# A two-layer encoder on eight cores: sine table in small steps, weights in smaller pieces, a new store layout, and fewer waits at the end

## The chip, the cores and the metric

One Trainium2 chip, eight cores, one sequence of the batch on each; no core waits for another. The time is device time of the slowest core in microseconds (us). A program on all eight cores has a slower state, whatever the kernel: in some executions the cores of one die, or of both, show a lower granted TensorE clock and take several per cent longer. The engines are called PE (TensorE), ACT (ScalarE), DVE (VectorE), POOL (GpSimd) and SP (SyncE); POOL and SP also issue the transfers, each on a ring of its own.

## The reference, cut to what matters

```python
# x: [8, 2048, 2048]; layer 0 gated linear attention, layer 1 latent attention
for i in range(2):
    y = gla_mixer(x, ...) if i == 0 else mla_mixer(x, positions, ...)
    x = layer_norm(alpha * x + y, ln_g[i], ln_b[i])

def gla_mixer(x, ...):      # 4 heads, chunks of 64 frames
    q, k, v, z, a_lr = split(x @ w_in)
    log_a = log_sigmoid(a_lr @ w_a2 + b_a) / 16
    state = decay * state + k^T v;  o = q state            # chunk by chunk
    return (rms_norm(o) * silu(z)) @ w_out

def mla_mixer(x, positions, ...):   # 16 heads; rotary part of 64, by sin/cos of position * inv_freq
    ...                             # chunk-causal softmax attention
    return (o * silu(z)) @ w_out
```

The sine and cosine of the positions are needed only in layer 1, which begins when the row tiles of layer 0 are done (after some 1050 us).

## The kernel before

The kernel is written as a list of operations; a scheduler in Python, with a cost model of engines and transfers, puts them in order on the five engines. An engine's queue is run in that order.

The sine table of 2048 positions is made in four blocks at the very start of the list, with a bonus in priority of 600, from one buffer for the positions (`trg`) and two for the result (`tra`):

```python
tra = [P.sbuf("tra", ..., [2, 512], F32) for j in range(2)]

def trig(tb, after=()):
    posi, ang, tk, ti = trg
    full = tra[tb % 2]
    P.dma(SP, posi, pos_d[:, tb * 512:(tb + 1) * 512], after=after)
    P.copy(ang, posi)
    P.ts(ang, ang, ropec[:, 0:1], None, ALU.mult)
    for f, shift in enumerate((0.0, PI / 2)):
        ...                              # nine DVE steps of 128x512: range reduction
    P.act(full, full, AF.Sin)            # ACT
    for f in range(2):
        P.dma(SP, cs_s[tb][f], full[:, f, :], ...)   # to HBM, for layer 1
```

At the end of layer 0 the output projection reads one row tile (`ogt`, 128 of the 2048 positions) per 64 matmuls, while the weights of the next stage (`wckv`) are loaded in two pieces of 1 MB. In layer 1 each head's output is transposed on PE, copied by DVE to a staging buffer (`ogS`, four of them) and stored by SP; beside that, in one of four head groups, POOL loads the output weights:

```python
P.copy(ogS[nh % 4], t)                                                   # DVE
P.dma(SP, ogT_s[1][4 * qb:4 * qb + 4, :, head, :].rearrange("i p t -> p i t"), ogS[nh % 4], ...)
...
if g == 1:
    load_slab(wout2[qb], m_wout[qb], after=[lastexp[0]])                 # four slabs
```

At the end SP waits for the last transfer on every semaphore, one after another:

```python
for o in last.values():                 # 120 of them
    h.wait_ge(nd[o.sem], o.cnt)
```

The softmax here doesn't subtract the row's maximum and nothing guards it: scores larger than these inputs give would overflow.

## Time and profile before

| | before |
|---|---|
| time, median of the first 4 runs | 2347.21 us (2277.78 to 2676.58) |
| profiled run (fast) | 2277.78 us |
| cores 0, 3, 4, 6 | 2275.0, 2276.2, 2275.5, 2273.0 us |
| cores 1, 2, 5, 7 | 2255.3, 2255.2, 2255.1, 2253.5 us |
| PE busy, slowest core | 96% |
| last matmul to the end, core 3 | 2259.9 to 2276.2 us |

The first four runs held slow ones, so their median says little; in all 18 runs taken beside the changed kernel the median is 2278.07 us. Read the profile as a stream of 12880 matmuls with a few holes in it: PE is the bound, so the question is only where it stands still and what it stands for. The prediction shows those lines. One line that it did not look at belongs here, the DRAIN at the end of POOL's queue on core 3, an instruction that every engine's queue ends with (name, count, duration in ns three times, first and last start):

```profile
L400 POOLq DRAIN  x1: 8664/8664/8664, 2265.3 to 2265.3; - x1
```

It is over at 2273.98, 2.3 us before the end: it costs nothing here.

### The profile page before, as it was taken

Reading aid. Unit: us, or ns where it says so; the run is one execution under the profiler, and the core shown is the slowest. Engines: PE = TensorE matmul, PEld = TensorE weight load, DVE = VectorE, ACT = ScalarE, POOL = GpSimd, SP = SyncE. Lnnn points to the kernel's source line nnn. Section 1 sums busy time; section 2 is a strip of 40 time slices with the busy share of each in tenths; the row PEclk is TensorE's granted clock in tenths of the full one; section 3 lists DMA queues with packets and bytes.
Section 4 is the critical chain, followed back from the end, with each engine's and each line's share of the span. In section 5 each row is a group of like instructions: output and inputs, shape, how many; then the busy total and the mean of one; then the engine's idle time right before and its main releaser. Section 6 shows DMA issues by size and latency. Waiting matters only on the chain.

```text
span 2276.2 us, 32728 instructions; the slowest of 8 cores (2253.5 to 2276.2 us)
## 1 busy us (share of the span) xinstructions
PE 2184.6 (96%) x12880; PEld 1100.2 (48%) x12880; DVE 978.0 (43%) x1819; ACT 836.0 (37%) x1539; POOL 344.4 (15%) x275
## 2 busy tenths in 40 slices
PE   6399999999999999999999999999989999999997
PEld 2144444444444444444444444446656666545553
DVE  1553444444344445666433222215343443565556
ACT  0354445444444442332432111114635555312220
POOL 2010111110111102333201111110000000032223
PEclk9799999999999999999999999999999999999998
DMA  9820600420152255545924344342266322434333
GB/s 162 153 65 10 128 12 10 82 58 10 28 107 49 49 142 150 183 156 182 185 58 113 101 124 129 100 138 75 61 146 141 91 65 77 165 141 147 134 126 121
DMA packets 132246, 237.59 MB, mean 104 GB/s; under 512 B 42368, under 2 KB 100096, under 8 KB 120832
## 3 DMA queue, kind: packets, MB, share of 16 engines
q1 hardware_dynamic: 119712, 164.20, 22.5%
q0 software_dynamic: 12384, 71.29, 18.4%
q8 instruction: 106, 1.74, 0.3%
q14 instruction: 44, 0.36, 0.1%
HBM read 229.15 MB, written 77.59 MB: 135 GB/s over the span
## 4 chain that ended last, share of the span: by engine, by line
PE 92%; DMA 5%; DVE 1%; ACT 1%; issue 0%; POOL 0%; DVEq 0%; SPq 0%; POOLq 0%
PE psum_all L153 89%; PE psum_all L159 2%; DMA trg<-pos_bc 2%; DMA ogT_s<-ogS 1%; DMA cs_s<-tra 1%; DMA xT<-xT 1%; DMA ogt<-ogT_s 1%; DVE slot_ap L188 0%; DVE xrE L188 0%; ACT L179 0%; ACT sig L179 0%; ACT tra L179 0%; DVE tra L188 0%; DVE trg L212 0%; ACT glp L179 0%
## 5 line engine op out<-in xcount | busy, mean ns | idle before, releaser
L153 PE MATMUL psum_all<-wsl,xT 128*128 128x512 bf16 x2048 | 471.6, 382 | 21.5 <-DMA wsl<-g_slab 19.9
L179 ACT ACTIVATE pT<-psum_all 128x1024 bf16<-128x1024 f32 (+1 forms) x320 | 284.6, 895 | 361.8 <-PE psum_all L153 361.2
L153 PEld LDWEIGHTS psum_all<-wsl,xT 128*128 128x128 bf16 x2048 | 195.8, 99 | 243.7 <-issue 36.4
L153 PE MATMUL psum_all<-wout,ogt 128*128 128x512 bf16 x1024 | 235.4, 382 | 5.3 <-DMA ogt<-ogT_s 5.3
L153 PE MATMUL psum_all<-xT,wsl 128*128 128x512 bf16 x1024 | 231.9, 379 | 0.0
L153 PE MATMUL psum_all<-wz,x1T 128*128 128x512 bf16 x1024 | 230.3, 379 | 0.0
L153 PE MATMUL psum_all<-wout,ogtE 128*128 128x512 bf16 x1024 | 226.3, 379 | 0.0
L153 PE MATMUL psum_all<-qnD,kC 128*128 128x512 bf16 (+3 forms) x640 | 221.5, 348 | 0.0
L153 PE MATMUL psum_all<-qrD,kr 128*128 128x512 bf16 (+3 forms) x640 | 218.6, 348 | 0.0
L153 PEld LDWEIGHTS psum_all<-vC,pT 128*128 128x128 bf16 x2176 | 148.6, 98 | 69.6 <-issue 0.7
L153 PE MATMUL psum_all<-vC,pT 128*128 128x129 bf16 x2176 | 179.8, 220 | 0.0
L153 PEld LDWEIGHTS psum_all<-wz,x1T 128*128 128x128 bf16 x1024 | 100.2, 98 | 120.8
L153 PEld LDWEIGHTS psum_all<-wout,ogtE 128*128 128x128 bf16 x1024 | 99.3, 98 | 117.5 <-issue 0.8
L153 PEld LDWEIGHTS psum_all<-wout,ogt 128*128 128x128 bf16 x1024 | 98.1, 98 | 113.5 <-issue 9.6
L188 POOL TENSOR_TENSOR slot_ap<-zs,gout 128x512 bf16<-128x512 bf16 x64 | 74.9, 1171 | 512.7 <-DVE zs L188 512.6
L153 PEld LDWEIGHTS psum_all<-xT,wsl 128*128 128x128 bf16 x1024 | 98.2, 98 | 110.3
L188 POOL TENSOR_TENSOR xrE<-xrE,lnbE 128x1024 f32<-128x1024 f32 (+1 forms) x31 | 84.2, 2737 | 421.3 <-DVE xrE L188 421.1
L179 ACT ACTIVATE zst<-psum_all 128x512 bf16<-128x512 f32 x64 | 38.2, 597 | 251.5 <-PE psum_all L153 251.5
L188 POOL TENSOR_TENSOR xr<-xr,lnb 128x1024 f32<-128x1024 f32 x32 | 88.3, 2777 | 145.5 <-DVE xr L188 145.5
L195 DVE SCALAR_TENSOR_TENSOR state<-state,cc,psum_all 128x512 f32<-128x512 f32 x112 | 78.7, 743 | 62.8 <-PE psum_all L153 59.3
L212 DVE CAST vC<-psum_all 128x512 bf16<-128x512 f32 x64 | 44.3, 692 | 118.2 <-PE psum_all L153 118.2
L175 ACT CAST slot_ap<-psum_all 128x512 bf16<-128x512 f32 x64 | 36.8, 586 | 133.1 <-PE psum_all L153 132.7
(142 smaller groups left out, 2590.8 us busy)
## 6 DMA issues: line engine op xcount, KB each, us to landing
wsl<-g_slab POOLq DMA_DIRECT2D x18, 1024.0 KB, 11.0
xr<-x SPq DMA_DIRECT2D x16, 1024.0 KB, 6.6
x_s<-xr SPq DMA_DIRECT2D x32, 512.0 KB, 3.5
xrE<-x_s SPq DMA_DIRECT2D x16, 1024.0 KB, 7.6
out<-xrE SPq DMA_DIRECT2D x30, 512.0 KB, 2.6
ogT_s<-ogst SPq DMA_DIRECT2D x64, 128.0 KB, 1.8
wout<-g_wout POOLq DMA_DIRECT2D x8, 1024.0 KB, 13.0
ogt<-ogT_s SPq DMA_DIRECT2D x16, 512.0 KB, 3.9
```

The source lines that it names most:

```text
L153: return self.add(PE, lambda: t.matmul(out, lhsT, rhs, start=start, stop=stop, skip_group_check=skip), [lhsT, rhs], [out], n / 2.4 + 3, af ...
L159: return self.add(PE, lambda: t.transpose(out, in_, idn), [in_, idn], [out], 56)
L175: f = lambda: a.copy(out, in_)
L179: f = lambda: a.activation(out, in_, func, bias=bias, scale=scale)
L188: return self.add(e, lambda: h.tensor_tensor(out, a, b, op), [a, b], [out], self.dcost(n) if e == DVE else 110 + 2.05 * n, after=after)
L195: return self.add(DVE, lambda: v.scalar_tensor_tensor(out, in0, s, in1, op0, op1), reads, [out], self.dcost(n))
L212: return self.add(e, lambda: h.tensor_copy(out, in_), [in_], [out], 130 + n * (0.65 if e == DVE else 1.2))
```

## The change

Its intent: take the sine work out of the way of the stream's start, take the pressure off the transfers at two places where PE waits, and shorten the end. Cut to its core:

```diff
 # scheduler's model of a transfer issued by SP
-    spfree = max(free[e] + 1200, spfree) + o.nbytes / 170.0
-    bwfree = max(bwfree, spfree) if bwfree < free[e] else bwfree + o.nbytes / self.BW
+    busy = bwfree > free[e] + 500
+    spfree = max(free[e] + 1200, spfree) + o.nbytes / (110.0 if busy else 300.0)
+    if busy:
+        bwfree += o.nbytes / self.BW
 # end: four waits after the last store, the others before it
-    for o in last.values():
+    for o in final[-4:]:
         h.wait_ge(nd[o.sem], o.cnt)
 # sine table: one operation at a time
-def trig(tb, after=()):
+def trig_steps():
+    ...                                   # the same operations, a yield after each
-P.bias = 600
-for t4 in range(4):
-    trig(t4, [ld])
-P.bias = 0
+trig = trig_steps()
 ...                                       # in head 0, per half-tile step from token block 1 on
+                if h == 0 and tb > 0:
+                    anchor = next(q.i for q in reversed(P.ops) if q.e == PE)
+                    n0 = len(P.ops)
+                    for _ in range(4):
+                        next(trig, None)
+                    for q in P.ops[n0:]:
+                        q.deps.add(anchor)
 # layer 0's row tiles: the loads of x split from those of ogt and issued earlier (cut)
 # next stage's weights in eight pieces
-            load_slab(wckv, m_slab[1])
+        if 3 <= i < 11:
+            q = 2 * (i - 3)
+            P.dma(POOL, wckv[:, q:q + 2, :], m_slab[1][:, q:q + 2, :], after=[P.ops[-1]])
 # layer 1's outputs: six staging buffers, one 1 KB row per partition
-    ogS = [... [4, 128] ... for j in range(4)]
+    ogS = [... [512] ... for j in range(6)]
-        P.dma(SP, ogT_s[1][4 * qb:4 * qb + 4, :, head, :].rearrange("i p t -> p i t"), ogS[nh % 4],
+        P.dma(SP, ogT_s[1][qb, :, head, :], st,
 # layer 1's output weights: 16 pieces over two head groups
-            if g == 1:
-                load_slab(wout2[qb], m_wout[qb], after=[lastexp[0]])
+        if g in (1, 2) and pr[0][0] == 0 and hh % 2 == 0:
+            n = 8 * (g - 1) + 2 * qb + hh // 2
+            P.dma(POOL, wout2[n // 4][:, 4 * (n % 4):4 * (n % 4) + 4, :], ..., after=[lastexp[0]])
```

With the sine part the load of the fourth weight slab (a block of 2 MB), whose place in memory the sine buffers use until then, moves from head 0's first token block to its last (cut here).

More of the change, by code (lines that the diff above doesn't have):

```diff
@@ L368, in ref @@
                 return (nd[d.sem] if d.dma else esem[d.e]), d.cnt
+            final = [o for o in self.order if o.dma and not o.succ]
             def body(e):
@@ L373, in run @@
                         w = {}
+                        if final and o is final[-4]:
+                            for f in final[:-4]:
+                                h.wait_ge(nd[f.sem], f.cnt)
                         for d in o.waits:
@@ L391, in run @@
                     if e == SP:
-                        last = {}
-                        for o in self.order:
-                            if o.dma:
-                                last[o.sem] = o
-                        for o in last.values():
+                        for o in final[-4:]:
                             h.wait_ge(nd[o.sem], o.cnt)
@@ L442, in build_program @@
     out_d = nc.dram_tensor("out", [NT, 128, D], F32, kind="ExternalOutput").ap()
-    ogT_s = [dscr(f"ogT{l}_s", [NT, 128, KC, 128], BF16) for l in range(2)]
+    ogT_s = [dscr("ogT0_s", [NT, 128, KC, 128], BF16), dscr("ogT1_s", [4, 128, KC, 512], BF16)]
     x1_s = dscr("x1_s", [NT, 128, D], F32)
@@ L682, in build_program @@
     tra = [P.sbuf("tra", W[2] + 8192 + 4096 * j, [2, 512], F32) for j in range(2)]
-    def trig(tb, after=()):
+    def trig_steps():
         posi, ang, tk, ti = trg
-        full = tra[tb % 2]
-        P.dma(SP, posi, pos_d[:, tb * 512:(tb + 1) * 512], after=after)
-        P.copy(ang, posi)
-        P.ts(ang, ang, ropec[:, 0:1], None, ALU.mult)
-        for f, shift in enumerate((0.0, PI / 2)):
-            a2 = full[:, f, :]
-            P.ts(a2, ang, shift, None, ALU.add)
-            P.ts(tk, a2, 1.0 / TWO_PI, None, ALU.mult)
-            P.copy(ti, tk)
-            P.copy(tk, ti)
-            P.stt(a2, tk, -TWO_PI, a2, ALU.mult, ALU.add)
-            P.ts(tk, a2, PI, -TWO_PI, ALU.is_gt, ALU.mult)
-            P.tt(DVE, a2, a2, tk, ALU.add)
-            P.ts(tk, a2, -PI, TWO_PI, ALU.is_lt, ALU.mult)
-            P.tt(DVE, a2, a2, tk, ALU.add)
-        P.act(full, full, AF.Sin)
-        for f in range(2):
-            P.dma(SP, cs_s[tb][f], full[:, f, :], dw=[("cs", tb)])
+        P.dma(SP, posi, pos_d[:, 0:512])
+        for _ in range(12):
+            yield
+        for tb in range(4):
+            full = tra[tb % 2]
+            P.copy(ang, posi)
+            yield
+            P.ts(ang, ang, ropec[:, 0:1], None, ALU.mult)
+            if tb < 3:
+                P.dma(SP, posi, pos_d[:, (tb + 1) * 512:(tb + 2) * 512])
+            yield
+            for f, shift in enumerate((0.0, PI / 2)):
+                a2 = full[:, f, :]
+                P.ts(a2, ang, shift, None, ALU.add)
+                yield
+                P.ts(tk, a2, 1.0 / TWO_PI, None, ALU.mult)
+                yield
+                P.copy(ti, tk)
+                yield
+                P.copy(tk, ti)
+                yield
+                P.stt(a2, tk, -TWO_PI, a2, ALU.mult, ALU.add)
+                yield
+                P.ts(tk, a2, PI, -TWO_PI, ALU.is_gt, ALU.mult)
+                yield
+                P.tt(DVE, a2, a2, tk, ALU.add)
+                yield
+                P.ts(tk, a2, -PI, TWO_PI, ALU.is_lt, ALU.mult)
+                yield
+                P.tt(DVE, a2, a2, tk, ALU.add)
+                yield
+            P.act(full, full, AF.Sin)
+            for f in range(2):
+                P.dma(SP, cs_s[tb][f], full[:, f, :], dw=[("cs", tb)])
+            yield
@@ L750, in build_program @@
             prev = (h, tb)
-            if h == 0 and tb == 0:
+            if h == 0 and tb == 3:
+                for _ in trig:
+                    pass
                 load_slab(sl_w(3), g_slab[3])
@@ L767, in __init__, with load @@
             self.nb = 0
-        def load(self, i):
+        def load(self, i, what="ox"):
             l = self.layer
-            P.dma(SP, self.ogt[i % len(self.ogt)], ogT_s[l][i], dr=[(f"ogT{l}", i, h) for h in range(4 if l == 0 else 16)])
-            P.dma(SP, self.xr[i % len(self.xr)], self.src[i], dr=[("x1", i)] if l else [])
+            src = ogT_s[1][i // 4][:, :, (i % 4) * 128:(i % 4) * 128 + 128] if l else ogT_s[0][i]
+            if "o" in what:
+                P.dma(SP, self.ogt[i % len(self.ogt)], src, dr=[(f"ogT{l}", i, h) for h in range(4 if l == 0 else 16)])
+            if "x" in what:
+                P.dma(SP, self.xr[i % len(self.xr)], self.src[i], dr=[("x1", i)] if l else [])
         def proj(self, i, n):
@@ L822, in build_program @@
     xr = [P.sbuf("xr", S + 8192 * j, [D], F32) for j in range(3)]
-    P.dma(SP, lng, lng_d[0])
-    P.dma(SP, lnb, lnb_d[0])
     ln0 = LN(0, x_d, x1_s, wout, lng, lnb, xr, ogt, stats, [0, 1])
@@ L845, in build_program @@
     ln0.load(0)
+    P.dma(SP, lng, lng_d[0])
+    P.dma(SP, lnb, lnb_d[0])
+    ln0.load(1, "x")
     for i in range(NT):
         if i + 1 < NT:
-            ln0.load(i + 1)
+            ln0.load(i + 1, "o")
         for n in range(4):
@@ L856, in build_program @@
                 x1_transposes(i - 1)
+            if n == (1 if i else 3) and i + 2 < NT:
+                ln0.load(i + 2, "x")
         ln0.norm(i)
@@ L1035, in build_program @@
     ogD = [P.sbuf("ogD", S + 16384 + 1024 * j, [4, 128], BF16) for j in range(4)]
-    ogS = [P.sbuf("ogS", S + 20480 + 1024 * j, [4, 128], BF16) for j in range(4)]
-    rsD = [P.sbuf("rsD", S + 24576 + 64 * j, [2], F32) for j in range(4)]
+    ogS = [P.sbuf("ogS", S + 20480 + 1024 * j, [512], BF16) for j in range(6)]
+    rsD = [P.sbuf("rsD", S + 27648 + 64 * j, [2], F32) for j in range(4)]
     o[0] = M
@@ L1160, in og_out @@
             P.tr(t[:, s, :], ogD[nh % 4][:, s, :])
-        P.copy(ogS[nh % 4], t)
+        st = ogS[nh % 6]
+        P.copy(st, bankb(b)[:, 0:512])
         head = 4 * g + hh
-        P.dma(SP, ogT_s[1][4 * qb:4 * qb + 4, :, head, :].rearrange("i p t -> p i t"), ogS[nh % 4],
+        P.dma(SP, ogT_s[1][qb, :, head, :], st,
               dw=[("ogT1", 4 * qb + s, head) for s in range(4)])
@@ L1242, in build_program @@
         p = scores(g, qb, hh, pr)
+        if g in (1, 2) and pr[0][0] == 0 and hh % 2 == 0:
+            n = 8 * (g - 1) + 2 * qb + hh // 2
+            P.dma(POOL, wout2[n // 4][:, 4 * (n % 4):4 * (n % 4) + 4, :], m_wout[n // 4][:, 4 * (n % 4):4 * (n % 4) + 4, :],
+                  after=[lastexp[0]])
         inflight.append((w, p))
```

## The prediction

> **What bounds the kernel now.** I read the page first, then the cores, then what TensorE (PE) waited for, and only then the stretches in which those waits lie.
>
> ```profile
> PE 2184.6 (96%) x12880; PEld 1100.2 (48%) x12880; DVE 978.0 (43%) x1819; ACT 836.0 (37%) x1539; POOL 344.4 (15%) x275
> PE   6399999999999999999999999999989999999997
> PEclk9799999999999999999999999999999999999998
> ```
>
> PE is busy 96% of the 2276.2 us, at full clock but for one slice near the start and the last one. The change removes no matmul, so all it can win is the other 92 us and what the clock loses after a gap. The waits of PE on this core (core 3, the slowest) say where those are:
>
> ```profile
> PE psum_all L153 <- ACT slot_ap L175: 34.5, 1, 34.5
> PE psum_all L153 <- DMA wsl<-g_slab: 19.9, 5, 12.8
> PE psum_all L153 <- DVE ogS L212: 9.6, 1, 9.6
> PE psum_all L153 <- DMA ogt<-ogT_s: 5.3, 1, 5.3
> ```
>
> Four entries are 69 us; the tail after the last matmul (2260 to 2276) is 16 more. The first 12.8 us of the weight wait is the start itself, which stays. The timeline around 100 us tells what the 34.5 us are:
>
> ```profile
> 97.97 0.43 DVE L202 TENSOR_SCALAR tra<-trg 128x512 f32<-128x512 f32 x1 [8.38 <-DMA cs_s<-tra]
> 100.69 1.06 ACT L179 ACTIVATE tra<-tra 128x1024 f32<-128x1024 f32 x1 [19.14 <-DVE tra L188]
> 101.66 2.03 ACT L175 CAST slot_ap<-psum_all 128x512 bf16<-128x512 f32 x4
> 102.85 5.72 PE L153 MATMUL psum_all<-xT,walr 128*16 128x512 bf16 x16 [34.49 <-ACT slot_ap L175]
> ```
>
> The rotary sine table stands in ScalarE's (ACT) queue ahead of the copies that empty PE's banks. ACT waited 19.14 us for VectorE (DVE), which waited for the store of the table before last, because there are two table buffers. PE had ended its third block at 68.4 us and got its bank only at 102.85.
>
> Cores 0, 3, 4 and 6 take 2273 to 2276 us, the other four 2253 to 2255. Core 1's waits start with
>
> ```profile
> PE psum_all L153 <- ACT slot_ap L175: 27.4, 1, 27.4
> ```
>
> and have 2.6 us for ogt and none for ogS. So the slow four carry two waits that the fast four hardly have, and the change must help the slow ones.
>
> **What the Trainium skill says.** (1) "TensorE: Matmul & The Clock Gate", Part 1: after an idle window of about 3.4 us PE falls to half clock and needs about as long to come back. The trace agrees: the windows after the ogt and ogS waits have granted clocks of 0.52 and 0.50:
>
> ```profile
> 875.00:880.00 5.00, 3.82 (x10) 1.34 (x11) 0.00 (x0) 0.00 (x0) 0.22 (x1) 0.52 0.85 320
> 1695.00:1700.00 5.00, 4.25 (x20) 2.28 (x21) 3.09 (x9) 0.42 (x1) 0.00 (x0) 0.50 1.01 293
> ```
>
> So each wait of over 3.4 us costs some 2 to 3 us on top of itself. (2) The same page, "Engine queue depths": ACT's and DVE's queues are strict FIFO; the 34.5 us are that. (3) "DMA: Bandwidth & Descriptors", "Queues, rings and completion order": each DMA engine takes turns between the rings it has work for, so SyncE's (SP) small transfers slow POOL's weight loads and the reverse; from 29 to 81 us the trace has POOL's ring at 93.0% and SP's at 12.0% of the engines. (4) "ScalarE: Activation LUTs", "What ACT_TABLE_LOAD costs": about 1283 ns for the load. The trace has 1.28 us, one load on each side of a Sin.
>
> **The change, part by part** (core 3).
>
> *The sine table* is cut into 84 small DVE steps, four per half-tile step of head 0's second and third token block, each held back to a PE instruction. The instruction order shows no Sin left before the bank copies. The copies follow the third block: two take about 1.2 us, as 101.66 to 102.85 shows, so PE resumes at 69.6. Then 16 low-rank matmuls at 0.216 us (3.4), the gate hop (0.8), two gate matmuls (0.4): 74.2. The 64 q/k matmuls need the third weight slab, and here a new wait may arise: its last piece was issued at 13.2 and took 68.2 us to land:
>
> ```profile
> L229 POOL DMA_DIRECT2D wsl<-g_slab x3: 707/715/723, 12.1 to 13.2; - x3
> DMA to landing us min/median/max: 59.5/65.0/68.2
> ```
>
> That is 81.4. The position loads and table stores (about 1.0 of the 1.51 MB that SP moved in that stretch) now go later, so 1.0/1.51 of 12% of 52 us, about 4 us, come off: 77.4. PE wants that piece at 74.2 + 12 x 0.216 = 76.8, so it waits 1 us at most. It ends the q/k tiles at about 88.7, where the trace has 123.4 (which contains 2.3 us of half clock: 16 matmuls in 5.72 us for 3.45). Gain 34.7.
>
> Against it: the third and fourth block now share DVE with the steps. One trig block is about 10 us of DVE (18 steps of 0.35 to 0.7 us, and two), 41 in all, over two token blocks of 39 and 48 us in which DVE was busy 18 to 22 us per block. That is 80 to 95% of DVE, still under PE. Four Sins with two table loads (3.6 us each) fall into a stage with ACT about half busy; three PSUM banks in rotation give some 7 us of slack. I charge 3 us.
>
> *ogS*: the output transposes get six staging buffers for four, one 1 KB run per partition in place of four of 256 B, and the output weights come in 16 pieces over two head groups. In the trace two 2 MB slabs (as bf16) were issued at 1662 and 1677 and a store took 26.5 us to land:
>
> ```profile
> 1668.61 26.48 DMA ogT_s<-ogS
> ```
>
> The pieces halve that rate, so the 9.6 us should go, and with them 3.1 us of half clock (0.50 for 5 us, 0.88 for 5). I count 12.
>
> *ogt*: PE asks for the third row tile's input 6.9 us after the load may start (32 matmuls); it took 12.25 us beside a 1 MB piece of the next weights and landed late:
>
> ```profile
> 863.80 12.25 DMA ogt<-ogT_s
> 876.18 6.46 PE psum_all L153 x16
> ```
>
> The piece shrinks to 0.26 MB. Without company this load takes 3.9 us (the issue table). So 5.3 plus 3.0 (6.46 for 16 x 0.216) is to be had; I count 7.
>
> *The end*: SP reads 120 semaphores in turn after the last store,
>
> ```profile
> L397 SPq EVENT_SEMAPHORE  x120: 17/17/17, 2269.7 to 2276.0; - x120
> ```
>
> The last store was issued at 2269.3 and lands after about 2.3 us, at 2271.7. With four waits left the end is 4.3 us sooner; the other waits are done earlier, when SP is idle.
>
> *The altered scheduler model* only reorders. PE's order up to the q/k tiles is the same, later it is interleaving. I charge nothing.
>
> Sum for core 3: 34.7 - 3 + 12 + 7 + 4.3 = 55. For core 1: 27.4 + 1 (clock, less the bank copies) - 1 (slab) - 3 + 2 + 4.3 = 31. They end at 2221 and 2224; the slowest core decides: about 2224, in a run's time with its 1.5 us above the span 2226.
>
> **The rivals.** *DMA takes over at the start.* If the slab lands no sooner than 81.4, or PE meets a gap over 3.4 us and cools, the q/k tiles end at 93 to 95 and 5 us go: 2232. For it: the DMA share is 1.0 up to 103 us. Against: three position blocks are out of the way. *DVE or ACT becomes the bound of head 0.* If the steps delay the bank-emptying ops, or a Sin stands before a gate's exp, PE loses 1 to 2 us per tile over some 20 tiles: 20 us back, 2246. For it: 80 to 95% is close, and the scheduler's costs know no table load. Against: each step is under 0.75 us and the gain is spread over 90 us. *The layout moves its cost to the loads.* The last layer's input tile becomes 2048 runs of 256 B where it was 128 of 4 KB. Even four times the 3.4 us to landing is 13.6, one row tile is 13.8 us, and three buffers give two tiles of lead: hidden, unless SP's ring backs up (one issue took 15.7 us at 1676). Then 5 to 10 us come back: 2234. *The slow cores gain nothing on ogS* because a load, not the weights, delays the stores: 2234.
>
> **Range and chances.** The border of 2% is 45.6 us. My gain is 55 on the slow cores, but the measure is the slowest of eight, and the middle value is 51. One rival coming true leaves 40 to 47. Runs of before that aren't slow span 2278 to 2300, so the level itself moves by 1%. Predicted 2227 us, 8 in 10 from 2206 to 2258. Faster by over 2%: 0.66; within: 0.32; slower: 0.02, as nothing is added to PE's path.
>
> **What would show it.** The wait on ACT slot_ap falls from 34.5 to about 1 us, with at most 3 us on the slab; no wait on ogS; ogt under 1.5 us; PE's last half-clock stretch is the start's; the wait line at the end shows 4 semaphores; all eight cores lie within 10 us. I am wrong if head 0 shows PE waits on DVE or ACT of over 8 us together, if PE waits for the last layer's input tile, or if PE's busy time grows.

## The result, and the profile after

The changed kernel took 2247.15 us in the median of 11 runs (2223.05 to 2664.4), the kernel before 2278.07 in the median of 18. That median is no good measure: 4 of the 11 runs were slow, and two, at 2247.15 and 2247.72, had two cores of one die at a clock of 0.983. The undisturbed runs are 2223.05 to 2224.17. Ratios here are the mean time of one kernel's fast runs over that of the other's of the same rounds, so not quite the ratio of the medians quoted: it is 0.9782, interval 0.9743 to 0.9822, which spans the border of 2%; the undisturbed runs alone lie 2.4% under 2278.07. The profiled run took 2223.76 us, and all its cores lie between 2219.4 and 2222.1.

The page of the changed kernel (core 2, its slowest): busy time and share of the engines, PE's busy tenths in 40 slices, and the granted clock.

```profile
PE 2177.5 (98%) x12880; PEld 1097.0 (49%) x12880; DVE 976.3 (44%) x1819; ACT 841.0 (38%) x1540; POOL 352.8 (16%) x289
PE   6999999999999999999999999999999999999997
PEclk9999999999999999999999999999999999999998
```

The hole in the second slice is gone, the dent at three quarters of the span too, and the clock does not fall in the second slice any more. PE's waits on core 3 (us in total, times, longest):

```profile
PE psum_all L153 <- DMA wsl<-g_slab: 20.5, 5, 13.0
PE psum_all L159 <- DVE og L195: 3.0, 2, 1.9
PE psum_all L153 <- DVE slot_ap L188: 1.5, 9, 0.2
PE psum_all L153 <- ACT a_lrT L175: 1.3, 2, 0.8
PE psum_all L153 <- ACT kk L175: 1.0, 1, 1.0
PE psum_all L153 <- ACT slot_ap L175: 0.6, 1, 0.6
```

That is the whole list. The 34.5 us on ACT are 0.6; ogS and ogt are not in it. What PE still waits for is the first weights, and small things. The timeline line that answers to the one at 102.85 us before:

```profile
66.59 3.61 PE L153 MATMUL psum_all<-xT,walr 128*16 128x512 bf16 x16 [0.61 <-ACT slot_ap L175]
```

Since both kernels run 12880 matmuls, I number them by start time and subtract: the lead of the changed kernel over the one before at the same number shows where each microsecond came from. The order of matmuls differs in places, so a point can be off by some tenths of a us; of those below only no. 5000 is (0.6 us too much lead). Core 3, us:

```
matmul no.   before   after    lead   what lies before it
   160         60.7     58.7    2.0   start: first weights
   272        122.9     84.6   38.4   sine table's wait, first q/k tiles
   700        208.9    173.0   36.0   head 0
  3500        758.6    722.8   35.9   heads 1 to 3
  4200        901.1    856.1   45.0   row tiles of layer 0 (ogt)
  5000       1050.3   1005.1   45.1
  6000       1234.1   1190.7   43.4   last row tiles of layer 0, layer 1's projections
  8600       1671.6   1628.1   43.5
  8800       1706.9   1651.2   55.7   attention, second group (ogS)
 12880       2259.9   2204.3   55.6   last matmul
   end       2276.2   2219.8   56.5
```

The steps are +36.4 (sine), -2.5 (head 0), +9.1 (ogt), -1.6 (a new small loss), +12.2 (ogS) and +0.9 (end), with 2.0 from the first weights' landing, which differs from run to run. Of the 9.1 some 0.8 is not ogt: two short stops of PE near 808 us, 1.04 us long before and in experiments 8 and 9, take 0.25 here. The -1.6 can be placed too. In layer 0's row tiles PE stops for some 0.26 us ahead of a tile's transposes of x1, until ACT has cast it (at 1016.07 us in one case; the transposes start at 1016.21). That happens 15 times here and 9 times in the kernel before and in experiments 8 and 9, which have the old scheduler model. The six more, between 986 and 1061 us, make 1.6 us; each is too short for the list of waits. Core 1, a fast core before, has +29.5 (5.1 to 34.6), -2.2, +3.0, -1.6, nothing for ogS, and +0.9 at the end: 34.6 in all.

Two lines are not as predicted. At the end of core 3 SP's four waits are over at 2216.0, but the kernel ends at 2219.8:

```profile
L400 SPq EVENT_SEMAPHORE  x4: 17/17/17, 2214.1 to 2216.0; - x4
L403 POOLq DRAIN  x1: 9802/9802/9802, 2209.7 to 2209.7; - x1
L403 POOLq EVENT_SEMAPHORE  x2: 17/17/17, 2219.6 to 2219.7; - x2
```

POOL's drain runs from 2209.73 to 2219.53, and only then do all engines leave. It is also longer than before, 9.80 us for 8.66. And within head 0, PE's longest new wait (1.92 us, for og) stands behind a Sin with its two table loads on ACT:

```profile
162.19 1.28 ACT L179 ACT_TABLE_LOAD   x1
163.48 1.06 ACT L179 ACTIVATE tra<-tra 128x1024 f32<-128x1024 f32 x1
164.56 1.28 ACT L179 ACT_TABLE_LOAD   x1
...
168.59 0.75 DVE L195 SCALAR_TENSOR_TENSOR og<-psum_all,ss,slot_ap 128x512 bf16<-128x512 f32 x1 [0.45 <-ACT ss L179]
...
169.49 0.38 PE L159 MATMUL psum_all<-ident,og 128*128 128x128 bf16 x4 [1.92 <-DVE og L195]
```

By the order of time, ACT's 3.6 us push its own sums of squares (ss) back, DVE waits for those, PE for DVE.

### The profile page after: what moved, and what is told of

It reads as the page before. It is cut to its first block, busy times and chain, and to the rows that moved or that the text cites. A ratio compares the mean times of both kernels' runs of the same rounds, so it can differ in the third digit from the quotient of the medians.

```text
span 2222.1 us, 32671 instructions; the slowest of 8 cores (2219.4 to 2222.1 us)
## 1 busy us (share of the span) xinstructions
PE 2177.5 (98%) x12880; PEld 1097.0 (49%) x12880; DVE 976.3 (44%) x1819; ACT 841.0 (38%) x1540; POOL 352.8 (16%) x289
## 3 DMA queue, kind: packets, MB, share of 16 engines
q8 instruction: 106, 1.74, 0.3%
## 4 chain that ended last, share of the span: by engine, by line
PE 96%; DMA 2%; DVE 1%; ACT 1%; POOL 0%; issue 0%; DVEq 0%; SPq 0%; POOLq 0%
PE psum_all L153 93%; PE psum_all L159 3%; DMA wsl<-g_slab 1%; DVE slot_ap L188 0%; DVE xrE L188 0%; ACT L179 0%; DMA ogt<-ogT_s 0%; POOL xT L229 0%; ACT slot_ap L175 0%; POOL wsl L229 0%; ACT tra L179 0%; ACT sig L179 0%; DVE trg L212 0%; DVE tra L188 0%; ACT state_b L179 0%
```

## The experiments

Twelve kernels, in three calls; the kernel before ran beside each call at 2278.69, 2276.57 and 2279.61 us (medians). The calls ran on different chips, so times are compared within a call. The scheduler can put instructions in another order after any edit. In the traces of core 3 the orders on PE, ACT, DVE and SP are those of the kernel before in experiments 5, 6 and 7, where POOL's list alone differs or nothing does; experiment 10 has the order of 9, and experiment 11 that of 8 but for the two operations moved. In experiments 1, 3, 4 and 12 the order changes beyond the edit.

### 1 and 2: the sine work alone, and all but the sine work

`e1_sine_spread` is the kernel before with the sine part of the diff above; `e2_all_but_sine` is the changed kernel with that part undone.

```diff
 # e1: on the kernel before          # e2: on the changed kernel, reversed
-P.bias = 600; trig(0..3, [ld])
+trig = trig_steps(); four steps per half-tile step of head 0
```

> The kernel before with the sine table's work alone spread over head 0 (84 small steps), nothing else changed. Theory (each gap is separate and its share adds up): the wait of PE on ACT slot_ap falls from 34.5 us (core 3) to about 1, the waits on ogS (10 us, slow cores alone) and ogt stay, slow cores go from 2276 to about 2244, fast cores from 2255 to about 2229, the run to about 2246 us. Rival 1 (the slab of weights takes the wait over): PE waits over 5 us on the third slab and the run stays above 2250. Rival 2 (VectorE or ScalarE bound in head 0): over 8 us of PE waits on DVE or ACT between 90 and 200 us.

Measured: 2245.14 us (2244.27 to 2246.86), ratio 0.9854 (0.9838 to 0.987). On core 3 the wait on ACT is 0.6 us, the waits on ogS (11.9) and ogt (5.1) are still there. The lead table of this kernel reads +36.3 for the sine wait and -4.3 for head 0. In this run all eight cores waited for ogS, between 2.4 and 11.9 us, where four had not in the run before: that wait is no property of certain cores.

> The changed kernel with the sine table's work put back where it was before. Theory: the 26 to 35 us wait on ACT slot_ap is back on every core, no ogS wait, ogt under 1.5 us, end 4.3 us shorter: slow cores about 2253, fast cores about 2249, the run about 2254 us, and the two gains (this and the spread alone) add up to that of the whole change, 52 to 54 us. Rival (the gaps hide one another): the two gains add up to clearly less, or more, than the whole.

Measured: 2252.95 us (2250.95 to 2273.86; in the highest, which was profiled, cores 0 and 1 had a clock of 0.978), ratio 0.9908 (0.9859 to 0.9958). The time is as expected, but not for the expected reason. No core waits for ogS, and ogt costs at most 0.6 us. But with the old sine work in place the wait on ACT should have stayed at 26 to 34 us, and it is 12.6 us on core 3 and 12.6 to 21.1 on the others, with 3.8 to 6.9 us for DVE behind it. Something else in the change had already shortened it. So the two halves overlap, as the rival had it: 33.5 and 25.7 us make 59.2, and the whole change, taken on its profiled run, has 54.3.

### 3: four table buffers

The store of the table before last held up DVE. If the two table buffers are the whole cause, two more should do as much as the spreading.

```diff
-    tra = [P.sbuf("tra", W[2] + 8192 + 4096 * j, [2, 512], F32) for j in range(2)]
+    tra = [P.sbuf("tra", a, [2, 512], F32) for a in (W[2] + 8192, W[2] + 12288, S + 20480, S + 24576)]
-        full = tra[tb % 2]
+        full = tra[tb]
```

> The kernel before with four table buffers in place of two, sine work still at the start. Theory (head-of-line: VectorE's queue held steps that needed a buffer whose store was under way, and the copies of the PSUM banks stood behind the second Sin): the wait on ACT slot_ap falls from 34.5 us to under 6, the run is within 8 us of the spread alone. Rival (the work itself must leave the start, because VectorE and the DMA engines are too busy there): the wait stays above 20 us.

Measured: the fast runs are 2268.05 to 2269.94 us, ratio 0.9956 (0.9939 to 0.9974): a miss. Over half of the wait stays, 19.8 of 34.5 us on core 3. The timeline of core 3:

```profile
79.81 0.43 DVE L212 CAST trg<-trg 128x512 f32<-128x512 int32 x1 [8.05 <-DMA trg<-pos_bc]
...
83.21 1.06 ACT L179 ACTIVATE tra<-tra 128x1024 f32<-128x1024 f32 x1 [23.54 <-DVE tra L188]
...
89.85 6.38 PE L153 MATMUL psum_all<-xT,walr 128*16 128x512 bf16 x16 [19.84 <-ACT slot_ap L175]
```

DVE no longer waits for a store, but now for the load of the next positions, of which there is one buffer; these loads stand beside the weights of the start. The Sin still stands in ACT's queue ahead of the four copies that PE waits for. The 34.5 us thus come from the place of the Sin in ACT's queue at a time when transfers are slow; what the Sin waits for is exchangeable, and buffers buy only the difference between two waits. This is read from the timelines; a run in which the Sin alone moves behind the copies was not made.

### 4: the scheduler's model alone

```diff
-    spfree = max(free[e] + 1200, spfree) + o.nbytes / 170.0
+    busy = bwfree > free[e] + 500
+    spfree = max(free[e] + 1200, spfree) + o.nbytes / (110.0 if busy else 300.0)   # and bwfree
```

> The kernel before with the new DMA estimate in its scheduler alone. In the instruction order the second Sin still stands ahead of the four bank copies. Theory: the wait on ACT slot_ap stays between 25 and 36 us and the run within 0.3% of before (2271 to 2285 us). Rival (the reordering by the new estimate is what wins): over 10 us faster.

Measured: median 2290.1 us of 5 runs, ratio 1.0019 (0.996 to 1.0078), but in the profiled run cores 6 and 7 had a clock of 0.975; its other six cores took 2248.2 to 2265.7, so the undisturbed run of 2267.89 us is the one to read: some 10 us less than before. The expectation missed and its rival came true, though on this one run. On core 3:

```profile
85.96 1.06 ACT L179 ACTIVATE tra<-tra 128x1024 f32<-128x1024 f32 x1 [7.10 <-DVE tra L188]
...
88.13 6.20 PE L153 MATMUL psum_all<-xT,walr 128*16 128x512 bf16 x16 [16.38 <-ACT slot_ap L175]
```

With a model that thinks transfers beside others slower (110 for 170) the order of DVE's steps is another: ahead of this Sin DVE waits 1.27 us for a store, where it waited 7.34 and 8.38 us, and the same Sin runs at 85.96 where it ran at 100.69. The wait on ogt is gone too, 0.4 us at most on any core. This is what had shortened the wait in the second experiment.

### 5 and 6: the two halves of the ogS part

`e5_wout_pieces` is the kernel before with the weights in 16 pieces; `e6_store_layout` is the kernel before with six staging buffers and the 1 KB rows.

```diff
 # e5
-            if g == 1: load_slab(wout2[qb], m_wout[qb], after=[lastexp[0]])
+        if g in (1, 2) and pr[0][0] == 0 and hh % 2 == 0: P.dma(POOL, wout2[n // 4][:, 4 * (n % 4):...], ...)
 # e6
-    ogS: 4 buffers, ogT_s[1][4 * qb:4 * qb + 4, :, head, :]   (four rows of 256 bytes per partition)
+    ogS: 6 buffers, ogT_s[1][qb, :, head, :]                  (one row of 1 KB)
```

> The kernel before with one part of the change: the output weights of the last layer are loaded in 16 pieces over two head groups in place of four slabs of one group. Theory of the prediction (two 2 MB slabs stand beside the output transposes' stores, and so the stores land late): the wait of PE on ogS is gone on every core (under 1.5 us, where 4 of 8 cores of the kernel before had 8 to 10 us, and all 8 of the kernel with the spread sine work 2 to 12), all cores lie within some 8 us of each other apart from their ScalarE wait, and the time falls to about 2264 us. Rival (the four staging buffers or the short 256-byte rows of the stores are the cause): several cores keep 8 to 12 us on ogS and the time stays at 2278.

Measured: fast runs 2264.36 and 2265.07 us, ratio 0.9949 (0.9926 to 0.9973). No core waits for ogS, and the cores lie between 2255.3 and 2262.8 where the kernel before, in its profiled run, had two groups some 20 us apart. Between 1660 and 1695 us on core 3 POOL's ring takes 28.4% of the transfer engines' time, where it took 70.1%.

> The kernel before with one other part: the last layer's transposed outputs go out as one 1 KB row per partition in place of four of 256 bytes, from six staging buffers in place of four; the weights stay in four slabs. Theory of the prediction (the weights' traffic makes the wait): with six buffers the ring is given two more stores of slack but the stores still land late, so some cores keep a wait on ogS of 3 to 8 us and the time falls by under 8 us. Rival (buffers and short rows are the cause): no wait on ogS on any core and about 2264 us. If both this and the pieces alone clear it, the two are enough each.

Measured: 2277.04 us (2275.51 to 2698.66, the highest slow), ratio 1.0004 (0.998 to 1.0028). No core waits for ogS here either, and yet four cores take 2271.9 to 2274.0 us. The list of waits on core 0, one of the four, and its chain of work at that place (start, us, what):

```profile
PE psum_all L153 <- DVE ogD L195: 8.5, 1, 8.5
```

```profile
1664.83 28.57 DMA zD<-z_s
```

The wait has moved one step up. With two more staging buffers DVE does not wait for a store any more; it goes on to the next product (ogD), and that needs zD, a load on the same ring, which takes 28.57 us at the same place where the store had taken 26.48. So the stores' layout and buffers were not the cause. SP's ring is slow while the weights come in, and the first transfer that somebody needs is named in the profile. A buffer count that makes one line vanish while the time stays is a sign of that. The fifth experiment, which takes the weights' burst away, is the part of the change that works.

### 7: the next stage's weights in eight pieces

```diff
-            load_slab(wckv, m_slab[1])
+        if 3 <= i < 11:
+            P.dma(POOL, wckv[:, q:q + 2, :], m_slab[1][:, q:q + 2, :], after=[P.ops[-1]])
```

> The kernel before with the next layer's down-projection weights in eight pieces of 0.26 MB in place of two of 1 MB, and nothing else. Theory of the prediction (the 1 MB piece beside the load of the third row tile makes it late): the wait on ogt falls from 2.2 to 6.0 us on every core to under 1.5, and the slow cores' time by some 3 to 7 us, 2272 to 2275. Rival (it is the place of the load in the queue, which the scheduler's model sets: with the new model alone the wait was 0.4 us at most): it stays at 2 to 6 us and the time at 2278.

Measured: 2270.68 us (fast runs 2269.09 to 2272.04), ratio 0.9973 (0.9954 to 0.9993). No core waits for ogt any more, at the same scheduler model. So the pieces suffice, and so does the model alone (experiment 4); the rival, that the place in the queue is the cause, is another way to the same end rather than a contradiction. (With the new model SP issues this load at 854.98 us, before at 863.80.)

### 8: the whole change with the old model

```diff
 # on the changed kernel
-    busy = ...  (new model)
+    (old model)
```

> The whole change but for the scheduler's model of the transfers, which is the old one. If the model's part of the gain (it alone took 18 us off the ScalarE wait, and the wait on ogt) is only a part of what the spread sine work and the pieces do anyway: within 5 us of the whole change, 2223 to 2229 us on undisturbed cores, with no ScalarE wait of over 1 us and ogt under 1.5 us. If the model is needed for ogt: PE waits 2 to 6 us on ogt, and the time is 5 to 9 us longer.

Measured: 2222.67 us (fast runs 2222.27 to 2223.18), ratio 0.9765 (0.9748 to 0.9781): faster by over 2% with its whole interval, and 1 us below the changed kernel. It was run at another time. On core 3 it has the same leads within 0.8 us, but for the -1.6 between matmul 5000 and 6000, which it does not have; its last matmul is 1.4 us earlier. So the model, worth 10 us alone, is worth nothing beside the other parts, and costs 1.6 us by the short stops in layer 0's row tiles. Why its order puts those transposes too early was not pursued.

### 9 and 10: three parts alone, and the short end on top

`e9_three_parts` is the kernel before with the sine work spread, the output weights in 16 pieces and the next stage's weights in eight; `e10_three_parts_end` has the four waits at the end as well.

```diff
 # e9 = before + e1 + e5 + e7;  e10 = e9 and:
-    for o in last.values(): h.wait_ge(...)       # 120
+    for o in final[-4:]: h.wait_ge(...)          # 4, the others before the last store
```

> The kernel before with three parts of the change alone: the sine work spread, the output weights in 16 pieces, the next layer's down-projection weights in eight. Not: the staging buffers and the store layout, the order of the first layer's loads, the scheduler's model, the short waits at the end. Theory (these three hold the whole gain but for the end): one lead after another as in the whole change, some +36 us by the end of the first q/k tiles, -2.5 over head 0, +9 past ogt, +12 past ogS on the slow cores; no wait of over 1 us on ScalarE, ogS or ogt; 2224 us, within 2 us of the whole change. Rival (the layout or the order of the loads matters too): a wait of over 2 us on ogS, ogD, zD or ogt is left, and the time is 2228 or more.

Measured: 2224.01 us; of its four fast runs three are 2223.59 to 2224.01, one, at 2248.83, makes the interval wide (ratio 0.9795, 0.9738 to 0.9851). No core waits for ACT's bank copies, ogS, ogD, zD or ogt beyond 1 us. Steps of its lead on core 3: +36.3, -2.4, +8.3, +12.1. Three parts hold the whole gain; the store layout, the six buffers, the earlier loads and the model add nothing to the time that these runs show.

> The three parts with the short waits at the end: four semaphores after the last store in place of 120. The prediction counted 4.3 us for this. Theory formed from the traces: the end is then set by GpSimd's drain, which lasted 8.66 us with 86 transfers issued by GpSimd, 9.15 with 92, 9.31 with 94 and 9.80 with 100 (0.0816 us for each), and which the 120 waits had hidden; here, with 100, it is 9.80 us again, SyncE is done about 3.6 us before the last instruction, and the gain over the three parts is 0.8 to 1.2 us (1.2 = 120 waits ended 2.26 us after the drain with 86 transfers, less 14 x 0.082). Rival (the prediction's term): 3 to 4.3 us.

Measured: 2223.48 us (2223.15 to 2224.61), ratio 0.9757 (0.9743 to 0.9772). From the last matmul to the end core 3 takes 15.47 us for 16.34 without the short end: 0.87 us. On core 3 of this kernel:

```profile
L398 SPq EVENT_SEMAPHORE  x4: 17/17/17, 2215.8 to 2218.3; - x4
L401 POOLq DRAIN  x1: 9807/9807/9807, 2211.4 to 2211.4; - x1
```

SP is done 3.1 us before the end; the drain, over at 2221.24, is what the end waits for.

### 11: POOL's last work given to DVE

If POOL's drain sets the end, it must start sooner. In the last row tile POOL multiplies and adds gain and bias of one quarter; here DVE does.

```diff
 # on e8_whole_old_model, last row tile only
-                    e = POOL if n == 3 else DVE
+                    e = DVE
```

> The whole change with the old model, and with the last row tile's two GpSimd operations (gain and bias of one quarter) given to VectorE, so that GpSimd's last work is that of the row tile before, which ended at about 2201.5. Theory: its drain of 9.8 us is over at about 2211 and no longer sets the end; VectorE's gain and bias operations, which took 1.64 and 1.74 us beside GpSimd's and 0.68 alone, all take about 0.6 to 0.7, so the last store is issued about 1 us sooner though VectorE has two more; the end follows the last store's landing by 0.3 us: 4 to 5 us less than the whole change with the old model, about 2218 us. If the drain lasts until after SyncE's last wait whatever GpSimd did before: no gain, 2222 to 2223. If VectorE's two additional operations cost their full 1.3 us on the path and nothing else is sped up: 2220.

Measured: 2219.64 us (fast runs 2218.88 to 2219.85), ratio 0.9738 (0.9724 to 0.9753). From the last matmul to the end core 3 takes 10.95 us for the 15.47 of experiment 8. The end on core 3, and DVE's last operations:

```profile
L398 SPq EVENT_SEMAPHORE  x4: 17/17/17, 2213.8 to 2215.6; - x4
L401 POOLq DRAIN  x1: 12656/12656/12656, 2197.7 to 2197.7; - x1
```

```profile
2208.40 1.29 DVE L188 TENSOR_TENSOR xrE<-xrE,lngE 128x512 f32<-128x512 f32 x2
2209.61 1.29 DVE L188 TENSOR_TENSOR xrE<-xrE,lnbE 128x512 f32<-128x512 f32 x2
```

The drain, which is counted from within the row tile before, is over at 2210.39 and stands in nobody's way; the end is 0.3 us after SP's last wait. And DVE, with eight operations for six, ends sooner: 8.4 us after the last matmul, where it ended 9.3 us after it in experiment 8. In the changed kernel, beside POOL's own operations, the same DVE operations read:

```profile
2208.52 1.64 DVE L188 TENSOR_TENSOR xrE<-xrE,lnbE 128x512 f32<-128x512 f32 x1
...
2210.08 2.35 DVE L188 TENSOR_TENSOR xrE<-xrE,lngE 128x512 f32<-128x512 f32 x2
```

One took 1.64 us instead of 0.68, another (in the second line) 1.74. Each ended 0.55 us after one of POOL's two operations had ended, in experiment 8 as well. This agrees with the Trainium skill, "Advanced Engine Details and Errata", "GPSIMD Details", which states that Pool shares a read and a write interface with DVE and conflicts with DVE instructions that have two SBUF inputs. Work "given to the idle engine" cost the busy one more than it saved. This version takes 3 us less than experiment 8 and, as expected, 4.5 us less in the tail. It was run at another time. So the tail is the better measure.

### 12: without the sine table's DVE steps

Eighteen of the 20 DVE steps per block are left out, two fills stand for them; a wrong result. (The comparison with the reference would not notice a wrong table.)

```diff
-            for f, shift in enumerate((0.0, PI / 2)): ...   # 18 steps
+            P.memset(full[:, 0, :], 0.5, DVE); yield
+            P.memset(full[:, 1, :], 0.25, DVE); yield
```

> The whole change with 18 VectorE steps per table block left out in favour of two fills, so a wrong result on purpose; the Sin, the position loads, the first two steps and the stores stay. It asks what the spread steps cost PE in head 0: between the 272nd and the 700th matmul the whole change lost 2.4 us against the kernel before. Theory (the steps delay the operations that PE waits for: og, zs, kk): most of it comes back, PE's waits on og, kk and zs in head 0 fall by 1.5 to 2.5 us and the time by as much, to about 2221. Rival (the four Sins and their table loads, or the order, are the cause): those waits and the time stay within 0.7 us.

Measured: fast runs 2230.68 to 2230.93 us, slower than with the steps. Both theories missed. The instruction order tells why the run does not answer the question: with less work for DVE the scheduler placed PE's transposes of og earlier in PE's queue in most of the places where the two orders differ. On core 3 PE's waits on og grew from 3.0 to 6.5 us, and the lead fell by 6.7 us between matmul 272 and 1000. One of these waits:

```profile
113.70 1.06 ACT L179 ACTIVATE tra<-tra 128x1024 f32<-128x1024 f32 x1
...
116.30 0.75 DVE L195 SCALAR_TENSOR_TENSOR og<-psum_all,ss,slot_ap 128x512 bf16<-128x512 f32 x1 [2.98 <-ACT ss L179]
...
117.20 0.38 PE L159 MATMUL psum_all<-ident,og 128*128 128x128 bf16 x4 [2.21 <-DVE og L195]
```

With the steps gone DVE is free, and it waits 2.98 us for ACT, which is at the Sin and its table loads. So these waits come without the steps, and behind the Sin; how the 2.5 us of the changed kernel divide between Sin, steps and order stays open.

## Why the prediction was right, and where it was not

It said 2227 us; undisturbed runs are 2223.05 to 2224.17. For core 3 it had a sum of 55; measured are 56.5. That the sums are so near is in part luck: the end brought 3.4 us less than counted, which the chance of the first weights (2.0) and the larger gains of the sine table and ogt made up. By its terms:

- **Sine table, +34.7: measured +36.4.** PE resumes 0.6 us after its third block, not 1.2, since two bank copies overlap with the block's last matmuls; and the third slab is there when it is wanted, so the 1 us for it did not come. The rival, that the transfers become the bound there, is refuted: there is no wait for a slab in the q/k tiles.
- **Head 0's charge, -3: measured -2.5.** Right in size, though it lies between -1.2 and -4.3 in the other kernels with the same sine work (experiments 1 and 8 to 11). DVE was busy 84% of the time from 100 to 182 us, within the 80 to 95% counted. The rival with 20 us did not come true. The longest of the waits that are left stands behind a Sin, as shown above.
- **ogt, +7: measured +9.1**, of which 8.3 is ogt (as in the three parts alone): the 5.3 and 3.0 that it found to be had. The smaller piece does it, as argued, and experiment 7 shows it alone. On core 1, where I had counted 2, it is 3.0.
- **ogS, +12: measured +12.2.** The mechanism named, the weights' traffic, is right, and experiments 5 and 6 separate it from the other two measures of the change, which the prediction had put beside it without dividing the gain. The rival "a load, not the weights, delays the stores" falls with experiment 5. That the layout moves its cost to the loads falls too: no core waits for the last layer's input.
- **The end, +4.3: measured +0.9 (0.87 in experiment 10). This step failed.** The prediction counted from the last store's landing at 2271.7 to the end, and took SP's semaphores for all that lies between. The landing was right (last store issued at 2213.7, seen at 2215.97, 2.3 us). But another engine ended later: POOL's drain, which began when POOL's last operation did and had been over 2.3 us before the end. Taking 120 waits away lays it bare; and the change itself made it 1.14 us longer, with 14 more transfers on POOL. The line was in the profile before. The lesson is to ask for every engine when it is done, not only for the one that ends last.
- **The scheduler's model, 0: in the whole change -1.4 to -1.6, alone +10.** "It only reorders" was a poor reason: another order alone took the 34.5 us down to 16.4. The zero came out nearly right because the spread sine work leaves nothing for the model to win.
- **The clock.** The gain in half clock that it counted came: the granted clock is 1.00 from 30 to 2200 us.
- **"The slow four cores".** The waits were rightly told apart, but the cores are not fixed: which ones are slow changes from run to run.

Two terms were not in the sum: 2.0 us from the landing of the first weights, which is chance (on core 3 it lies between -1.6 and 2.1 in the other kernels with the spread sine work), and the 1.6 us lost before the transposes of x1. The changed kernel's ratio of 0.9782 includes two runs with a disturbed pair of cores.

## What to carry to other kernels

A wait in the list names the transfer that was needed first, not the reason why transfers are slow: add a buffer, and if the line vanishes and the time stays, look at who else is using the engines' rings. In a strict queue, work that is needed much later must not stand ahead of work that is needed now. Before shortening the end, list when each engine is done: the gain reaches only as far as the engine that is done last but one.

## What the Trainium skill lacked or had wrong

- "VectorE: DVE Perf Modes", "The DRAIN you can't avoid", knows two kinds of DRAIN: the flush after a DVE operation, and a boilerplate one of about 12 ns, constant on all five engines. Here the last ones on core 3 of the kernel before took 4.08 us on PE, 2.25 on ACT and 1.21 on DVE. POOL's lasted 8.66 us with 86 transfers issued by POOL in the whole kernel, 9.15 with 92, 9.31 with 94 and 9.80 with 100, on every core within 5 ns or so: 0.081 us more for each transfer more, and next to nothing else once POOL's last operation is over (8.25 us with 100, both in the changed kernel and in experiment 11). Each transfer had 144 packets on average in all of these, so a cost per packet is not told apart from one per transfer. SP's last DRAIN, after 538 transfers, took 7 ns. No page has this. Splitting a load in POOL's ring thus has a price at the end, unless POOL is done early.
- No page that I read tells how a loss falls on neighbouring cores (it belongs to "HBM Reference"). In 17 undisturbed runs of the kernel before, and three of experiment 6, each of the pairs 0/1, 2/3, 4/5 and 6/7 has a core of at least 2270 us; in 51 of these 80 pairs its neighbour is more than 12 us faster, and the roles change from run to run. What in the pair makes this was not tested.
